# Layer 0 of a two-layer diffusion trunk: a third PSUM bank for attention scores, and projection work tied to its place among the attention tiles

## The chip, the core and the metric

The kernel runs on one core of a Trainium2 chip. The core has a matrix engine (PE in the profile; its weight loads have a row of their own, PEld), a vector engine (DVE), a scalar engine (ACT), GpSimd (POOL), and SyncE (SP), which issues most of the DMAs. Every engine works through its own list of instructions in order, and engines wait for one another by semaphores. PE writes its results to PSUM, which has eight banks of 128 x 512 fp32 values.

The metric is the device time of one execution in microseconds, lower is better.

## The reference, cut to what matters

Two layers work on 1024 latent tokens and 256 context tokens with 1024 features. Layer 0 (an "even" layer) projects the normalised, modulated tokens to queries, keys, values and gates, runs two groups of attention heads side by side, multiplies by a SiLU gate, and projects back:

```python
def even_mixer(h_lat, h_ctx, w_in, w_out, q_gain, k_gain, sink, cos, sin, update_ctx):
    ...
    aq, ak, av, ag, bq, bk, bv, bg = project(h_lat)
    c_aq, c_ak, c_av, c_ag, c_bq, c_bk, c_bv, c_bg = project(h_ctx)
    aq, ak, bq, bk = (apply_rope(t, cos, sin) for t in (aq, ak, bq, bk))
    ...
    oa = lax.map(lambda qb: gqa_attend(qb, ka, va), qa_blk)      # A: all keys
    ...
    ob = lax.map(b_block, (jnp.arange(n_blk), qb_blk))           # B: context and a band of keys, with a sink
    ...
    y_lat = jnp.concatenate([oa * jax.nn.silu(ag), ob * jax.nn.silu(bg)], axis=-1) @ w_out
```

Layer 1 (an "odd" layer) holds a depthwise convolution of 31 taps with a layer norm, and a two-dimensional neighbourhood attention with a table of biases. A final RMS norm gives the output.

## The kernel before

All products are fp32 values split in a high and a low part, so each logical product is three matmuls (`mm3`, lines 318 to 320: high by high, high by low, low by high). Attention in layer 0 is cut in four units `u`, each one key head with four query heads. `ORDER = (2, 3, 0, 1)`: first the two windowed B units, then the two global A units. A unit has ten groups of 128 queries (two of context, eight of latent tokens); a group is a run of key tiles, two to five in B and two or ten in A. Units 2, 3, 0, 1 have 42, 42, 84 and 84 tiles. In this text tiles are counted through the program: 0 to 41 for unit 2, 42 to 83 for unit 3, 84 to 167 for unit 0, 168 to 251 for unit 1, and 252 to 363 for the 16 groups of seven tiles of layer 1.

One tile is this chain: PE forms the score `st` in a PSUM bank, with one matmul over `QH` (line 465) and a second one over `QL` (line 469); ACT takes the exponential (`pf`, line 477) and its high part `ph` (line 296); POOL, or every twelfth time DVE, makes the low part `pl` (line 299); PE adds three matmuls to the output `ov` (lines 409 to 411). `attn_gen` issues the `ov` products of a tile three tiles behind its score (`LOOK0`). `QL` holds, beside the low parts of the queries, the negated row maxima, and these come from a preparation that runs beside earlier groups: matmuls into `mx` (lines 576, 588, 596), a maximum by DVE over each, `nmt`, a transpose on PE into `trn` (line 387), and a multiplication by DVE that writes `QL` (line 388). So the first `QL` matmul of a group needs its `trn` and the DVE step behind it.

The other work of layer 0 is fill for PE between the tiles: `proj_qkv` of the next unit (`pq`, ten blocks of 24 matmuls, then transposes `trk` into the layout of the keys in `qk_tail`), `proj_gate` (`pg`), and for the finished units the output products (`po`, `out0_part`). `weave` advances the attention generator `main` by `nmain` steps, two for a tile, and deals `nfill` steps of `fill` evenly among them. What it deals out is only a trace: a scheduler then orders each engine's list by priority and by its own estimate of when operands are ready. In layer 0 fill is traced with a priority 80 places later (`FL`), so the scheduler may move it far. `tc.issue_after(x)` adds an edge that keeps an instruction behind `x` on the same engine; `weave` has a parameter `lag` for it, which layer 0 does not use. In layer 1 fill has a priority 98 places earlier, and two of its four weaves use `lag`.

PSUM banks are shared out by tag: two for `pp` (projections), two for `mx`, two for `st`, one for `ov`, one for `tr`, which serves all small transposes and column sums (`trn`, `trm`, `trs`). The tag of `trk` is `tr` as well.

Weights come by DMA into `wr`, two buffers deep in layer 0, are cast by ACT to `wh` (line 296) and get their low part `wl` from POOL (line 299). The cast stands in ACT's list among the exponentials.

Of the kernel before, what the change touches and what calls it, by code (L numbers as in the profile page):

```python
# [41 lines left out]
TRV = "pp"  # L42
# [6 lines left out]
N0 = 9  # L49
NLAST = (48, 28)  # L50
PFB = 2
# [4 lines left out]
FL = (80, -98)  # L56
# [11 lines left out]
LATE = 100  # L68
NFILL = (34, 34, 34)
HV = (('gggvvvvg',) * 3, ('gggvvvvg', 'vvvgvvvg', 'gggvvvvg'))  # L70
O1 = (6, 84, 46, 14)
TICK0, TICK1 = (1, 3)
# [15 lines left out]
def tile_kernel(ctx: ExitStack, tc: tile.TileContext, a, out):  # L88
# [7 lines left out]

    BUFS = {"pp": 2, "mx": 2, "st": 2, "ov": 1, "tr": 1}
    solo = [True]
    turn = [0, 0]
    mk, mwp, hold, layer = [0], [None], [0], [0]  # L100
    sts, pvs = [], []

    def bank(tag, name):
# [65 lines left out]
    def mod_half(pool, l, part, j):  # L169

        pb = bank("pp", nm("pm"))
        c0 = part * 1024 + j * 512
        for d2 in range(4):
            w2 = mw_tile()
            mm0.append(SY.dma_start(w2, a["mod_w"][l, 2 * d2 * P : (2 * d2 + 2) * P, c0 : c0 + 512].rearrange("(d p) n -> p d n", d=2)))
            for d in range(2):
                dk = 2 * d2 + d
                PE.matmul(pb[0:2, :], csil[:, dk, :], w2[:, d, :], start=(dk == 0), stop=(dk == DK - 1))
        row = a0.tile([P, 512], F32, tag="ost", name=nm("mrow"), bufs=2)[0:2, :]
        SC.copy(row, pb[0:2, :])  # L180
        tr = bank("tr", nm("trm"))
        for i in range(4):
            PE.transpose(tr[:, 2 * i : 2 * i + 2], row[:, i * P : (i + 1) * P], ident[0:2, 0:2])
        trv = tr[:, 0:8].rearrange("p (i c) -> p i c", c=2)
        o = part * 8 + j * 4
        dst = modT[l][:, o : o + 4, :]
        VE.tensor_tensor(dst, trv, modb[:, l, o : o + 4, None].broadcast_to([P, 4, 2]), op=ALU.add)
        if part == 1:
            VE.scalar_tensor_tensor(gs[l][:, j * 4 : j * 4 + 4, :], dst, 1.0,
                                    normg[:, l, j * 4 : j * 4 + 4, None].broadcast_to([P, 4, 2]),  # L190
                                    op0=ALU.add, op1=ALU.mult)

    def mod_half_v(pool, l, part, j, conds):
# [28 lines left out]
        for n_, (q, t) in enumerate(zip(conds, accs)):  # L222
            tr = bank("ov" if solo[0] else "tr", nm("trm"))
            for i in range(4):
# [18 lines left out]

    def rstd_steps(pool, accs, n, tag, inv=1.0, tr="tr"):

# [68 lines left out]

    done = [None]

# [47 lines left out]
    def attn_prep(pool, g):  # L364
# [19 lines left out]
        for _ in range(3):  # L384
            yield
        tr2 = bank("tr", nm("trn"))
        PE.transpose(tr2[0:nr, 0:P], nmt[:, 0:nr].bitcast(F32), ident)
# [4 lines left out]
    def attn_gen(pool, groups, vshare, look, nexts=None):  # L392
# [57 lines left out]
        for x, (g, t) in enumerate(items):  # L450
# [13 lines left out]
            cs = slice(k * P, (k + 1) * P)  # L464
            sts.append(PE.matmul(st[:, :n], KA[:, cs], g.QH[:, q0 : q0 + n], start=True, stop=False))  # L465
            if not g.bias:
# [27 lines left out]

    def weave(main, nmain, fill, nfill, last=True, all_fill=True, lag=0):

        done = 0
        for k in range(nmain):
            next(main, None)
            while done * nmain < (k + 1) * nfill:  # L500
                with ExitStack() as cx:
                    cx.enter_context(later(FL[layer[0]]))
                    if lag and len(sts) >= lag:
                        cx.enter_context(tc.issue_after(sts[-lag].ins))
                    next(fill, None)
                done += 1
        if all_fill:
            for _ in fill:
                pass
        if last:  # L510
            for _ in main:
                pass
# [139 lines left out]
    with ExitStack() as p0x:  # L652
# [6 lines left out]
        with tc.tile_pool(name="st0", bufs=1, reuse_waits="tile") as st0:  # L659
# [31 lines left out]
            def norm_bc(c, acc):  # L691
                n = CHUNKS[c][1]
                return run(rstd_steps(st0, [acc], n, "st"))[:, :n]

# [139 lines left out]
        def qk_tail(u, j, pc):  # L834

            tr = bank("tr", nm("trk"))
            for i in range(3):
# [45 lines left out]
        for k in range(3):  # L883
            u = ORDER[k]
            n = NSTEP[u // 2] + (12 if k == 0 else 0)
            n0 = 0 if k else N0
            if not k:
                weave(main, n0, proj_gate(u, gblocks(k)[1]), 9, False)
            weave(main, n - n0 - NLAST[u // 2], fill0(k + 1), NFILL[k], False)
            weave(main, NLAST[u // 2], proj_gate(ORDER[k + 1], gblocks(k + 1)[1]), 18, False)  # L890
        run(mods)
# [78 lines left out]
    with tc.tile_pool(name="o0", bufs=1, reuse_waits="tile", side="right") as op_:  # L970
# [91 lines left out]

        weave(main, O1[0], load_oh(parts[0]), 6, False)
        weave(main, O1[1], out0_part(parts[0]), 48, False)
        weave(main, O1[2], chain(load_oh(parts[1]), out0_part(parts[1])), 30, False)
        ws = [load_w(op_, a["ev_wo"], e2 * 256, 256, 256, WO, lambda dk: "gv"[dk % 2], dks=final, rb=2) for e2 in range(4)]
        fp = [final_proj(c) for c in range(3)]
        nh = [norm_h(0, "st", "tr"), norm_h(1, "pp", "tr"), norm_h(2, "st", "tr")]
        weave(main, NSTEP[U1 // 2] - O1[0] - O1[1] - O1[2], through_attention(), O1[3])
        a0x.close()  # L1070
# [28 lines left out]
    with ExitStack():  # L1099
# [25 lines left out]
        def ln_steps(vp, c):  # L1125
# [25 lines left out]
            yield  # L1151
            bc = yield from rstd_steps(vp, [s1], 512, "st", 2.0)
            SC.copy(s2, bc)
# [480 lines left out]
```

## Time and profile before

| | |
|---|---|
| median of 3 runs | 1557.82 us (1554.83 to 1560.38) |
| the profiled execution | 1555.72 us |
| its span on the core | 1553.9 us |
| mean granted PE clock | 0.967 |
| busy share PE, PEld, DVE, ACT, POOL | 93%, 75%, 72%, 49%, 54% |
| first score of layer 0 | 159.4 us |
| first score of unit 3, unit 0, unit 1 | 325.8, 471.4, 685.9 us |
| first score of layer 1 | 1213.3 us |

The page names the busy time of each engine. A windows view cuts the span into stretches and gives, for each, its length and then the busy time of PE, PEld, DVE, ACT and POOL with the number of instructions in brackets, then the granted PE clock (PEclk, 1.00 is full speed), the share of the DMA engines and GB/s. With a line chosen it counts the instructions of that line alone. A waits view gives the engine and the tile that waited, what released it, the total, the number of times and the longest, all in us.

### The profile page before, as it was taken

The numbers are of one execution on the slowest core, as the hardware profiler recorded it, in microseconds if no ns is written. First come the engines' busy times: TensorE is split into PE (matmuls) and PEld (weight loads), VectorE is DVE, ScalarE is ACT, GpSimd is POOL, SyncE is SP. The second block draws the span as 40 slices with busy tenths as digits, with TensorE's granted clock in tenths as the row PEclk, the third lists the DMA queues.
The fourth block names the chain that finished last, engine by engine and source line by source line (L and its number), as shares of the span: only waits on it lengthen the run. The fifth ranks groups of instructions, "written<-read, shape, count | busy, mean of one in ns | idle before, by whom it ended". The sixth has DMA issues, their size and how long they took to land.

```text
span 1553.9 us, 22052 instructions
## 1 busy us (share of the span) xinstructions
PE 1449.1 (93%) x6984; PEld 1172.3 (75%) x6984; DVE 1123.3 (72%) x2172; ACT 759.8 (49%) x1545; POOL 833.5 (54%) x762
## 2 busy tenths in 40 slices
PE   6989989999999989899999889999999999799995
PEld 1878868887789678678887668888787787687784
DVE  4998898689858666654577677999755457586776
ACT  2721354445454755565455555443434455545563
POOL 1561464555555676675455666664542443545574
PEclk9999999999999999999999999999999999899996
DMA  9548245423441124631111121213456888788623
GB/s 339 194 146 270 79 125 174 147 64 121 151 129 44 54 89 143 207 115 56 42 45 35 68 95 57 80 63 123 158 178 222 272 225 263 221 264 240 192 92 109
DMA packets 185614, 221.01 MB, mean 142 GB/s; under 512 B 17421, under 2 KB 139481, under 8 KB 185497
## 3 DMA queue, kind: packets, MB, share of 16 engines
q1 hardware_dynamic: 178832, 208.03, 43.1%
q10 hardware_dynamic: 6664, 11.57, 2.3%
q8 instruction: 55, 0.90, 0.2%
q14 instruction: 63, 0.51, 0.1%
HBM read 159.51 MB, written 60.03 MB: 141 GB/s over the span
## 4 chain that ended last, share of the span: by engine, by line
PE 67%; DVE 12%; DMA 11%; issue 3%; POOL 3%; ACT 2%; SPq 2%; DVEq 0%; ACTq 0%; POOLq 0%
PE p L320 6%; PE p L318 6%; PE p L319 6%; PE ov L409 4%; PE ov L410 4%; PE ov L411 4%; PE st L465 4%; PE po L318 4%; PE st L469 4%; PE po L319 4%; PE po L320 4%; PE pq L320 2%; PE pq L319 2%; PE pq L318 2%; DMA mw<-in_mod_w_dram 2%
## 5 line engine op out<-in xcount | busy, mean ns | idle before, releaser
L299 POOL TENSOR_TENSOR pl<-pf,ph 128x512 fp32r<-128x512 f32 (+4 forms) x321 | 399.9, 1258 | 270.7 <-ACT ph L296 218.9
L299 POOL TENSOR_TENSOR wl<-wr,wh 128x256 fp32r<-128x256 f32 (+2 forms) x256 | 197.7, 788 | 227.9 <-ACT wh L296 203.3
L477 ACT ACTIVATE pf<-st 128x512 f32<-128x512 f32 x284 | 166.2, 596 | 161.7 <-PE st L469 106.3
L296 ACT CAST ph<-pf 128x512 fp32r<-128x512 f32 (+4 forms) x364 | 209.2, 588 | 25.5 <-PE ov L410 17.6
L296 ACT CAST wh<-wr 128x256 fp32r<-128x256 f32 (+2 forms) x264 | 103.2, 404 | 172.2 <-DMA wr<-in_od_d_dram 39.3
L318 PE MATMUL p<-hh,wh 128*128 128x512 f32 x448 | 177.7, 399 | 3.7 <-DVE spk L299 1.4
L319 PE MATMUL p<-hl,wh 128*128 128x512 f32 x448 | 177.9, 398 | 0.2 <-POOL hl L299 0.2
L320 PE MATMUL p<-hh,wl 128*128 128x512 f32 x448 | 175.2, 399 | 0.1
L465 PE MATMUL st<-QH,KAt 128*128 128x512 f32 (+4 forms) x364 | 144.0, 397 | 19.8 <-ACT pf L477 16.5
L409 PE MATMUL ov<-ph,Vt 128*128 128x512 f32 (+4 forms) x364 | 143.6, 394 | 8.8 <-DVE y L631 6.4
L411 PE MATMUL ov<-pl,Vt 128*128 128x512 f32 (+4 forms) x364 | 143.7, 395 | 3.9 <-POOL pl L299 3.8
L410 PE MATMUL ov<-ph,Vt 128*64 128x512 f32 (+4 forms) x364 | 140.8, 387 | 0.0
L469 PE MATMUL st<-QL,KBt 68*128 68x512 f32 (+4 forms) x364 | 138.2, 388 | 0.8 <-DVE QL L388 0.7
L1116 DVE SCALAR_TENSOR_TENSOR cps<-U,taps,cps 128x512 f32<-128x512 f32 x184 | 124.3, 747 | 0.0
L589 DVE TENSOR_REDUCE mp<-mx 128x1 f32<-128x512 f32 x128 | 85.5, 682 | 33.5 <-PE mx L588 32.7
L219 DVE SCALAR_TENSOR_TENSOR macc<-mw,csil,macc 128x512 f32<-128x512 f32 x107 | 97.5, 929 | 14.0 <-DMA mw<-in_mod_w_dram 13.2
L318 PEld LDWEIGHTS p<-hh,wh 128*128 128x128 f32 x448 | 84.6, 189 | 24.5 <-DVE spk L299 1.6
L465 PEld LDWEIGHTS st<-QH,KAt 128*128 128x128 f32 x364 | 69.8, 192 | 42.5 <-ACT pf L477 25.3
L319 PEld LDWEIGHTS p<-hl,wh 128*128 128x128 f32 x448 | 84.6, 189 | 20.4 <-POOL hl L299 0.6
L320 PEld LDWEIGHTS p<-hh,wl 128*128 128x128 f32 x448 | 84.6, 189 | 20.3 <-POOL wl L299 1.0
L411 PEld LDWEIGHTS ov<-pl,Vt 128*128 128x128 f32 x364 | 71.1, 195 | 28.1 <-POOL pl L299 7.6
L409 PEld LDWEIGHTS ov<-ph,Vt 128*128 128x128 f32 x364 | 71.5, 196 | 24.3 <-issue 7.0
(277 smaller groups left out, 3518.4 us busy)
## 6 DMA issues: line engine op xcount, KB each, us to landing
mw<-in_mod_w_dram SPq DMA_DIRECT2D x34, 512.0 KB, 5.6
bs<-in_d_bs_dram SPq DMA_DIRECT2D x16, 832.0 KB, 7.3
Q<-qs SPq DMA_DIRECT2D x40, 256.0 KB, 2.7
QH<-Q SPq DMA_DIRECT2D x80, 128.0 KB, 2.7
bm<-in_d_bm_dram SPq DMA_DIRECT2D x16, 540.0 KB, 6.1
wr<-in_od_d_dram SPq DMA_DIRECT2D x64, 128.0 KB, 2.6
mw<-in_mod_w_dram SPq DMA_DIRECT2D x28, 256.0 KB, 3.1
wr<-in_ev_qkv_dram SPq DMA_DIRECT2D x32, 192.0 KB, 3.8
```

Source lines behind the costliest of these rows:

```text
L296: SC.copy(hi, src)
L299: (GP if leng == "g" else VE).tensor_tensor(lo, src, hi.bitcast(F32), op=ALU.subtract)
L318: PE.matmul(o, lh, rh, start=first, stop=False)
L319: PE.matmul(o, lh, rl, start=False, stop=False)
L320: done[0] = PE.matmul(o, ll, rh, start=False, stop=last)
L409: PE.matmul(o, V[:, 64:192], ph[:, :n], start=(t == 0), stop=False)
L410: PE.matmul(g.ov[0:64, q0 : q0 + n], V[:, 0:64], ph[:, :n], start=False, stop=False)
L411: pvs.append(PE.matmul(o, V[:, 64:192], pl[:, :n], start=False, stop=(last and g.sink is None)))
L465: sts.append(PE.matmul(st[:, :n], KA[:, cs], g.QH[:, q0 : q0 + n], start=True, stop=False))
L469: PE.matmul(st[:, :n], KB[0:68, cs], g.QL[0:68, q0 : q0 + n], start=False, stop=True)
L477: SC.activation(pf[:, :n], st[:, :n], AF.Exp, scale=1.0 if g.bias else SCALE)
L1116: VE.scalar_tensor_tensor(pc, uc, w, pc, op0=ALU.mult, op1=ALU.add)
```

## The change

1. PSUM: the `tr` bank is given up and `st` gets three banks. The small transposes and sums move: `trn`, the late `trm` and layer 0's and layer 1's `trs` to the `mx` banks, the early `trm` and the norms at the start to `st`, `trk` to the `pp` banks (`TRV`), the layer norm's sums to `st`.
2. Order: in layer 0 fill gets edges. With `lag`, a step of fill stays behind the `lag`-th last score; that is the loose form, with 8, used in the first two units. With `tie` as well, a score stays behind the product of the second last step of fill; with `lag` 4 and `tie` 2 this is used while unit 0 and unit 1 run, except in the last stretch of unit 1.
3. Dealing: the steps of `weave` are split anew. `NLAST` is now by unit, unit 0 gives up its last 36 steps (`SHIFT`) to the output products of the units done before, and eight steps of the last projection are issued ahead of its weave (`NPRE`).

```diff
-NLAST = (48, 28)
+NLAST = (28, 28, 56)
...
+HOLD, TIE, LOOSE = 4, 2, 8
+NPRE = (0, 0, 8)
...
-O1 = (6, 84, 46, 14)
+O1 = (6, 110, 66, 14)
+SHIFT = 36
...
-    BUFS = {"pp": 2, "mx": 2, "st": 2, "ov": 1, "tr": 1}
+    BUFS = {"pp": 2, "mx": 2, "st": 3, "ov": 1}
...
-        tr2 = bank("tr", nm("trn"))
+        tr2 = bank("mx", nm("trn"))
...
-            sts.append(PE.matmul(st[:, :n], KA[:, cs], g.QH[:, q0 : q0 + n], start=True, stop=False))
+            with ExitStack() as cx:
+                if tied[0] is not None:
+                    cx.enter_context(tc.issue_after(tied[0].ins))
+                sts.append(PE.matmul(st[:, :n], KA[:, cs], g.QH[:, q0 : q0 + n], start=True, stop=False))
...
-    def weave(main, nmain, fill, nfill, last=True, all_fill=True, lag=0):
+    def weave(main, nmain, fill, nfill, last=True, all_fill=True, lag=0, tie=0):
...
+        past = []
         for k in range(nmain):
+            tied[0] = past[-tie] if tie and len(past) >= tie else None
             next(main, None)
+            tied[0] = None
             while done * nmain < (k + 1) * nfill:
...
                     next(fill, None)
+                past.append(prods[0])
                 done += 1
...
-            tr = bank("tr", nm("trk"))
+            tr = bank(TRV, nm("trk"))
...
-            n = NSTEP[u // 2] + (12 if k == 0 else 0)
+            n = NSTEP[u // 2] + (12, 0, -SHIFT)[k]
...
-            weave(main, n - n0 - NLAST[u // 2], fill0(k + 1), NFILL[k], False)
-            weave(main, NLAST[u // 2], proj_gate(ORDER[k + 1], gblocks(k + 1)[1]), 18, False)
+            hold = dict(lag=HOLD, tie=TIE) if k == 2 else dict(lag=LOOSE)
+            fill = fill0(k + 1)
+            for _ in range(NPRE[k]):
+                with later(FL[0]):
+                    next(fill)
+            weave(main, n - n0 - NLAST[k], fill, NFILL[k] - NPRE[k], False, **hold)
+            weave(main, NLAST[k], proj_gate(ORDER[k + 1], gblocks(k + 1)[1]), 18, False, **hold)
...
-        weave(main, O1[1], out0_part(parts[0]), 48, False)
-        weave(main, O1[2], chain(load_oh(parts[1]), out0_part(parts[1])), 30, False)
+        weave(main, O1[1], out0_part(parts[0]), 48, False, lag=HOLD, tie=TIE)
+        weave(main, O1[2], chain(load_oh(parts[1]), out0_part(parts[1])), 30, False, lag=HOLD, tie=TIE)
...
-        nh = [norm_h(0, "st", "tr"), norm_h(1, "pp", "tr"), norm_h(2, "st", "tr")]
-        weave(main, NSTEP[U1 // 2] - O1[0] - O1[1] - O1[2], through_attention(), O1[3])
+        nh = [norm_h(0, "st", "mx"), norm_h(1, "pp", "mx"), norm_h(2, "st", "mx")]
+        weave(main, NSTEP[U1 // 2] + SHIFT - O1[0] - O1[1] - O1[2], through_attention(), O1[3])
...
-            bc = yield from rstd_steps(vp, [s1], 512, "st", 2.0)
+            bc = yield from rstd_steps(vp, [s1], 512, "st", 2.0, "st")
```

The number and the shapes of the matmuls stay the same; only their order and their banks differ. Three places of PE's list show it. In the rows, the number behind a name tells tiles apart, and line numbers of the new kernel are a few higher (322 to 324 for the three products of `mm3`, 472 and 476 for the two matmuls of a score, 413 to 415 for `ov`, 391 for `trn`, 587 and 599 for `mx`).

Unit 0, tiles 96 to 99. Before, PE's list holds scores, maxima and outputs there and no projection:

```order
L465 MATMUL st_5355<-QH_4845,KAt_3729 128x512
L469 MATMUL st_5355<-QL_4846,KBt_1254 128x512
L411 MATMUL ov_5154<-pl_5289,Vt_1255 128x512
L588 MATMUL mx_5226<-KAt_3729,QH_4995 128x512
L465 MATMUL st_5388<-QH_4845,KAt_3729 128x512
L469 MATMUL st_5388<-QL_4846,KBt_1254 128x512
L588 MATMUL mx_5232<-KAt_3729,QH_4995 128x512
L465 MATMUL st_5410<-QH_4845,KAt_3729 128x512
L469 MATMUL st_5410<-QL_4846,KBt_1254 128x512
```

After, in the same place, a score is followed by a step of nine `pq` matmuls:

```order
L472 MATMUL st_5498<-QH_4845,KAt_3729 128x512
L476 MATMUL st_5498<-QL_4846,KBt_1254 128x512
L322 MATMUL pq_5577<-wh_5009,hh_171 128x384
L323 MATMUL pq_5577<-wl_5010,hh_171 128x384
L324 MATMUL pq_5577<-wh_5009,hl_172 128x384
L322 MATMUL pq_5577<-wh_5015,hh_171 128x384
L323 MATMUL pq_5577<-wl_5016,hh_171 128x384
L324 MATMUL pq_5577<-wh_5015,hl_172 128x384
L322 MATMUL pq_5577<-wh_5021,hh_171 128x384
```

What moved is the projection: before, tiles 90 to 113 stand with 8 `pq` matmuls among them; after, 120 do, and the stretches of six tiles with hardly any fill are tiles 114 to 119 (none) and 144 to 149 (nine `pg`). In units 2 and 3 every stretch of six tiles now has fill, where before tiles 6 to 11 and 48 to 59 had none.

The start of the third latent group of unit 0, at tile 104. Before, the transpose `trn` of the group's maxima stands well ahead of the group:

```order
L387 MATMUL trn_5297<-ident,nmt_5271 4x128
L409 MATMUL ov_5402<-ph_5413,Vt_1255 128x512
L410 MATMUL ov_5402<-ph_5413,Vt_1255 64x512
L411 MATMUL ov_5402<-pl_5414,Vt_1255 128x512
L409 MATMUL ov_5402<-ph_5436,Vt_1255 128x512
L410 MATMUL ov_5402<-ph_5436,Vt_1255 64x512
L465 MATMUL st_5491<-QH_4845,KAt_3729 128x512
L469 MATMUL st_5491<-QL_4846,KBt_1254 128x512
```

(The group's own first score follows twelve rows further down.) After, at the same tile:

```order
L324 MATMUL pq_5801<-wh_5021,hl_172 128x384
L391 MATMUL trn_5415<-ident,nmt_5389 4x128
L587 MATMUL mx_5508<-KAt_3729,QH_5418 128x256 x2
L587 MATMUL mx_5525<-KAt_3729,QH_5418 128x256 x2
L476 MATMUL st_5689<-QL_5131,KBt_1254 128x512
L476 MATMUL st_5710<-QL_5131,KBt_1254 128x512
L476 MATMUL st_5731<-QL_5131,KBt_1254 128x512
L472 MATMUL st_5755<-QH_5130,KAt_3729 128x512
L476 MATMUL st_5755<-QL_5131,KBt_1254 128x512
```

The three `QH` matmuls of tiles 104 to 106 stand further up, and their three `QL` matmuls now come together, two `mx` tiles (four matmuls of 256 columns) behind the `trn` on which they depend. Of the 40 groups of layer 0, 15 have no more than four such matmuls between `trn` and the first `QL` matmul in the new order, and one had before.

Layer 1, tile 292. Before, the fill is used up and the list goes on with outputs:

```order
L465 MATMUL st_13848<-QH_13204,KAt_12379 128x224
L469 MATMUL st_13848<-QL_13205,KBt_12380 128x224
L1226 MATMUL trv_14451<-ident,vc_14446 128x128 x2
L409 MATMUL ov_13802<-ph_13695,Vt_12386 128x512
L410 MATMUL ov_13802<-ph_13695,Vt_12386 64x512
L411 MATMUL ov_13802<-pl_13696,Vt_12386 128x512
```

After, projection products (`p`) stand there:

```order
L472 MATMUL st_13848<-QH_13204,KAt_12379 128x224
L476 MATMUL st_13848<-QL_13205,KBt_12380 128x224
L323 MATMUL p_3499_14080<-hl_9771,wh_13967 128x512
L324 MATMUL p_3483_14008<-hh_9770,wl_13980 128x512
L322 MATMUL p_3483_14008<-hh_9770,wh_13985 128x512
L323 MATMUL p_3483_14008<-hl_9771,wh_13985 128x512
```

What moved in layer 1: tiles 292 to 303 had no `p` matmul and now have 105; tiles 252 to 259 had 97 and now have 6.

More of the change, by code (lines that the diff above doesn't have):

```diff
@@ L101, in tile_kernel @@
     sts, pvs = [], []
+    tied = [None]
     def bank(tag, name):
@@ L180, in mod_half @@
         SC.copy(row, pb[0:2, :])
-        tr = bank("tr", nm("trm"))
+        tr = bank("st", nm("trm"))
         for i in range(4):
@@ L222, in mod_half_v @@
         for n_, (q, t) in enumerate(zip(conds, accs)):
-            tr = bank("ov" if solo[0] else "tr", nm("trm"))
+            tr = bank("ov" if solo[0] else "mx", nm("trm"))
             for i in range(4):
@@ L242, in newton_rsqrt, with rstd_steps @@
         return r
-    def rstd_steps(pool, accs, n, tag, inv=1.0, tr="tr"):
+    def rstd_steps(pool, accs, n, tag, inv=1.0, tr="mx"):
         nb = n // P
@@ L313, in make_h @@
                 split(x, h[0][:, dk, :], h[1][:, dk, :])
-    done = [None]
+    done = prods = [None]
     def mm3(o, lh, ll, rh, rl, first, last):
@@ L692, in norm_bc @@
                 n = CHUNKS[c][1]
-                return run(rstd_steps(st0, [acc], n, "st"))[:, :n]
+                return run(rstd_steps(st0, [acc], n, "st", tr="st"))[:, :n]
             made = [0]
```

## The prediction

> **What bounds the kernel now.** The page comes first.
>
> ```profile
> PE 1449.1 (93%) x6984; PEld 1172.3 (75%) x6984; DVE 1123.3 (72%) x2172; ACT 759.8 (49%) x1545; POOL 833.5 (54%) x762
> ```
>
> PE sets the pace, and the change leaves its work as it is, so it can gain only the time in which PE stands still or runs at a lower clock. I read the windows view next, cut where runs of projection matmuls begin and end. The columns are stretch, length, busy PE, PEld, DVE, ACT, POOL, then PEclk.
>
> ```profile
> core 0: us, PE busy (x) PEld busy (x) DVE busy (x) ACT busy (x) POOL busy (x), PEclk, DMA share, GB/s
> 470.00:505.00 35.00, 35.00 (x185) 31.66 (x184) 30.10 (x53) 13.66 (x25) 18.82 (x15) 1.00 0.16 49
> 505.00:544.00 39.00, 35.45 (x152) 24.52 (x151) 23.60 (x47) 28.64 (x50) 26.79 (x21) 1.00 0.18 54
> 544.00:556.00 12.00, 12.00 (x66) 11.19 (x65) 10.07 (x19) 6.17 (x13) 9.99 (x9) 1.00 0.28 90
> 556.00:580.00 24.00, 19.15 (x75) 13.33 (x74) 13.88 (x27) 13.77 (x28) 15.05 (x14) 0.86 0.27 80
> 580.00:637.00 57.00, 57.00 (x283) 46.25 (x282) 38.48 (x68) 32.91 (x59) 39.73 (x28) 1.00 0.42 134
> 637.00:652.00 15.00, 12.79 (x47) 8.54 (x46) 11.90 (x22) 8.97 (x14) 10.31 (x7) 0.89 0.86 260
> 652.00:685.00 33.00, 29.34 (x137) 22.72 (x138) 15.55 (x28) 21.55 (x40) 24.43 (x23) 1.00 0.58 183
> 685.00:875.00 190.00, 189.88 (x900) 152.47 (x899) 125.05 (x224) 97.73 (x185) 107.47 (x91) 1.00 0.17 55
> ```
>
> The same stretches with line 318 alone, the first of the three products of all fill:
>
> ```profile
> 505.00:544.00 39.00, 0.00 (x0) 0.00 (x0) 1.00 0.18 54
> 556.00:580.00 24.00, 0.00 (x0) 0.03 (x1) 0.86 0.27 80
> 637.00:652.00 15.00, 0.00 (x0) 0.00 (x0) 0.89 0.86 260
> 685.00:875.00 190.00, 53.43 (x148) 27.66 (x147) 1.00 0.17 55
> ```
>
> With fill evenly dealt, as from 685 to 875 us, PE idles 0.12 us in 190. Without fill it idles 3.55, 4.85 and 2.21 us in 78, though no other engine is full. The waits view of 470 to 685 us names the largest wait of PE, and one that sits behind it:
>
> ```profile
> PEld st L465 <- ACT pf L477: 11.1, 8, 2.7
> ACT wh L296 <- DMA wr<-in_ev_g_dram: 8.1, 5, 4.2
> ```
>
> The timeline shows how they meet (PE rows first, then ACT's):
>
> ```profile
> 557.78 0.40 PE L469 MATMUL st<-QL,KBt 68*128 68x512 f32 x1
> 558.02 0.39 PE L588 MATMUL mx<-KAt,QH 128*128 128x512 f32 x1
> 560.61 0.50 PE L465 MATMUL st<-QH,KAt 128*128 128x512 f32 x1 [2.19 <-ACT pf L477]
> 563.07 0.51 PE L576 MATMUL mx<-KAt,QH 128*128 128x256 f32 x2 [1.21 <-DVE mp L589]
> 565.24 0.63 PE L465 MATMUL st<-QH,KAt 128*128 128x512 f32 x1
> ...
> 559.14 0.40 ACT L296 CAST wh<-wr 128x256 fp32r<-128x256 f32 x1 [4.23 <-DMA wr<-in_ev_g_dram]
> 559.45 0.61 ACT L296 CAST ph<-pf 128x512 fp32r<-128x512 f32 x1
> 559.97 0.59 ACT L477 ACTIVATE pf<-st 128x512 f32<-128x512 f32 x1
> ```
>
> A weight cast stands in ACT's list ahead of an exponential and waits 4.23 us for its DMA; both score banks are full; PE stands 2.19 us, and what follows runs at a lower clock (0.63 us a matmul against 0.40). Fill, or a third bank, would cover this.
>
> **Part 1, unit 0 (470 to 685 us).** The three stretches without fill lose 3.55 + 4.85 + 2.21 = 10.6 us of idling, and by the clock 0.14 x 24 + 0.11 x 15 = 5.0: 15.6 us. The scores in them are
>
> ```profile
> 505.00:544.00 39.00, 9.49 (x23) 4.32 (x23) 1.00 0.18 54
> 556.00:580.00 24.00, 4.36 (x9) 1.94 (x9) 0.86 0.27 80
> 637.00:652.00 15.00, 2.86 (x6) 1.23 (x6) 0.89 0.86 260
> ```
>
> 38 tiles, 0.41 us each. In the new order 12 tiles of unit 0 have next to no fill: 12 x 0.41 = 4.9 us stay. From 652 to 685 us output products have begun but 3.66 us are idle; I give the even dealing half, 1.8. Gain 15.6 - 4.9 + 1.8 = 12.5 us. The least is 6 (half), the most all 19.3.
>
> Idling as PE's rows show it may understate the loss, because a matmul's row (0.39) is longer than the step to the next (558.02 - 557.78 = 0.24). By weight loads, full PE means 152.47 / 190 = 0.80, so the three stretches did 24.52 + 13.33 + 8.54 = 46.4 us of loads, worth 58 us, in 78: 20 lost instead of 15.6. The Trainium skill (Perfetto Trace Analysis, Identifying the Most-Contended Engine) has this as a rule: judge PE by weight loads, since matmul busy time hides pipelining. By that rule the sum below would end 4.5 us lower; the trace agrees in direction, and since the mix of shapes sets the 0.80 too, I keep the idle time.
>
> **Part 2, units 2 and 3 (182 to 470 us).**
>
> ```profile
> 182.00:212.00 30.00, 26.26 (x116) 18.48 (x115) 27.53 (x65) 18.87 (x44) 17.34 (x14) 0.89 0.24 71
> 238.00:341.00 103.00, 101.84 (x546) 89.29 (x545) 77.33 (x167) 46.16 (x98) 52.47 (x42) 1.00 0.44 134
> 341.00:372.00 31.00, 27.19 (x122) 18.76 (x121) 28.34 (x66) 17.81 (x41) 17.82 (x14) 1.00 0.28 83
> 384.00:394.00 10.00, 7.98 (x39) 5.74 (x39) 9.82 (x18) 5.29 (x15) 5.72 (x6) 1.00 0.41 123
> 394.00:470.00 76.00, 73.39 (x376) 61.98 (x375) 52.39 (x110) 36.00 (x74) 42.30 (x35) 0.98 0.44 136
> ```
>
> The stretches of 30, 31 and 10 us, almost without fill, lose 3.74 + 3.81 + 2.02 us and 0.11 x 30 = 3.3 by the clock: 12.9. But here DVE is over 90% busy, where it is 75% and 69% in the two filled ones. Spreading fill spreads DVE's load too, yet the loose edges still let a group's maxima bunch up. I take 8, with ends 0 and 13.
>
> **Part 3, the price at group starts.** In 15 of 40 groups the new order puts `trn` at most two `mx` tiles ahead of the first `QL` matmul. The chain is in the timeline:
>
> ```profile
> 539.24 0.27 PE L387 MATMUL trn<-ident,nmt 128*4 128x128 f32 x1
> 539.54 0.68 DVE L388 TENSOR_TENSOR QL<-trn,k_bd 4x512 fp32r<-4x512 f32 x1 [1.52 <-PE trn L387]
> ```
>
> From `trn` to the end of DVE's step are 0.98 us, and PE starts 0.05 after a releaser (560.61 against 559.97 + 0.59). Between stand the `trn` (0.11, my estimate from its 128 columns) and four matmuls of 256 columns (half of 0.24 each): 0.59. So PE waits at least 0.44 us, and 0.68 more for each other DVE step queued ahead. Then three scores finish at once, and the fourth needs the first one's exponential (0.59). I take 0.6 us a group, 15 x 0.6 = 9 lost; the ends are 7 (the chain alone) and 45 (rival 1). `trn` in the `mx` banks and `trk` in the `pp` banks cost no work of their own; the attention matmuls around them hide their evacuation, else 0.68 a `trn` is part of that upper end.
>
> **Part 4, layer 1.** No edge is added here, but with the third bank the fill stands elsewhere.
>
> ```profile
> 1332.00:1362.00 30.00, 21.43 (x89) 15.99 (x88) 16.62 (x44) 15.95 (x34) 14.66 (x17) 0.77 0.88 235
> PEld mx L1342 <- DMA KAt<-KD: 3.5, 1, 3.5
> ```
>
> This stretch, tiles 292 to 303 in the main, loses 8.6 us idle and 0.23 x 30 = 6.9 by the clock: 15.5. The wait for a load of keys (3.5 us, second row, from the waits of this stretch) stays, with about as much for clock: 6.5. Tiles 252 to 262 lose their fill instead: 11 x 0.41 = 4.5. Gain 15.5 - 6.5 - 4.5 = 4.5; the ends are -5, if the old loss stays beside the new one, and 13.
>
> The start (to 159 us), the end of layer 0 and the tail have the same work in much the same order; I cost them at nothing, within 3 us either way.
>
> **The sum.** The profiled execution took 1555.7 us, 2.1 under the median. 1555.7 - 12.5 - 8 + 9 - 4.5 = 1539.7; with 2.1 added back, a median of **1542 us**, 1.0% faster.
>
> **Rivals.**
> 1. *Group starts become the bound: slower.* PE works strictly down its list, so nothing passes a waiting `QL` matmul. If DVE has three maxima (0.68 each) queued ahead, a start costs 0.44 + 2.0 + 0.59 = 3.0 us, 45 in all: 1555.7 - 25 + 45 = 1576, median 1578. It decides against the change above 25 / 15 = 1.7 us a group. For it: DVE at 92% without fill. Against: it is at 66% from 685 to 875 us. The clock matters here: two waits of 2.19 and 1.21 us close together brought PEclk to 0.86, while 3.55 us in small pieces left it at 1.00. The Trainium skill (TensorE: Matmul & The Clock Gate, The HAM clock gate) puts the limit at an idle window of about 3.4 us, by which single starts of 3 us would still cost no clock; the trace's case agrees only if the two waits count as one.
> 2. *The gaps only move.* Fill is a fixed amount; what one stretch gets another lacks (tiles 114 to 119, 144 to 149, 252 to 262). For it: ACT's weight casts still wait two buffers deep. Against: the 0.12 us above. With part 1 at its least and parts 2 and 4 at nothing: 1555.7 - 6 + 9 = 1559, median 1561.
> 3. *Full packing.* All of 19.3 + 13 + 13, and starts at 7: 1555.7 - 45.3 + 7 = 1517, median 1519. For it: the stretch from 685 to 875 us. Against: DVE's load in units 2 and 3.
>
> **How the numbers follow.** Forecast 0.66, rival 1 0.16, rival 2 0.10, rival 3 0.08. With each gain halfway to its ends (16 + 10.5 + 9, or 9 + 4 + 0) the forecast's own range is 1531 to 1554. Rival 3 opens the range to 1517, rival 2 to 1562; rival 1 is left out. About 0.3% (4.7 us) is what a measurement can tell from no change. Faster 0.66 + 0.08 = 0.74, same 0.10, slower 0.16.
>
> **What would show it.** Right: PE idle under 6 us in all of unit 0, PEclk 1.00 there, no ACT wait of over 2 us on a gate weight, and waits of `st` on DVE's `QL` near 9 us in total. Wrong: waits on `QL` or on maxima of over 25 us, or a layer 1 longer than before.

## The result, and the profile after

The changed kernel takes 1631.3 us (median of 4 runs, 1626.8 to 1634.2) against 1558.1 us (1554.8 to 1560.4) on the same chip: a ratio of 1.047, with a 95% interval of 1.0435 to 1.0503. The forecast was 1542 us, faster; the kernel is 73 us slower, above rival 1's 1578 too.

The profiled execution has a span of 1624.9 us, 71 longer. Its page has the same work, PE busy for 30 us more, at a mean granted clock of 0.946 against 0.967, and so idle for 41 us more:

```profile
PE 1479.4 (91%) x6984; PEld 1194.2 (73%) x6984; DVE 1127.6 (69%) x2172; ACT 763.4 (47%) x1545; POOL 836.2 (51%) x762
```

The windows view, cut at the first score of the program, of unit 0 and unit 1, at tile 246, at the first score of layer 1 and at the end, shows where. Columns: stretch, length, busy PE, PEld, DVE, ACT, POOL with counts, PEclk, DMA share, GB/s. First the kernel before:

```profile
159.00:472.00 313.00, 297.31 (x1517) 249.31 (x1516) 250.84 (x539) 149.19 (x332) 170.96 (x139) 0.98 0.39 120
472.00:686.00 214.00, 199.73 (x931) 157.18 (x931) 142.75 (x257) 124.67 (x225) 144.10 (x113) 0.98 0.37 115
686.00:889.00 203.00, 197.74 (x931) 157.48 (x930) 132.06 (x236) 106.06 (x200) 116.38 (x99) 0.99 0.16 50
889.00:1213.00 324.00, 314.08 (x1447) 253.93 (x1446) 236.73 (x391) 143.63 (x285) 174.96 (x179) 0.99 0.38 123
1213.00:1553.00 340.00, 305.48 (x1494) 249.18 (x1493) 233.43 (x547) 177.89 (x381) 168.98 (x178) 0.94 0.70 209
```

And after:

```profile
165.00:516.00 351.00, 309.03 (x1508) 259.45 (x1507) 244.00 (x535) 146.37 (x328) 169.72 (x137) 0.92 0.36 108
516.00:742.00 226.00, 209.67 (x966) 164.52 (x965) 146.98 (x257) 126.50 (x231) 150.72 (x120) 0.96 0.34 108
742.00:941.00 199.00, 194.13 (x903) 153.46 (x901) 129.00 (x233) 105.62 (x193) 110.53 (x92) 0.99 0.17 50
941.00:1277.00 336.00, 317.14 (x1433) 254.10 (x1432) 241.88 (x395) 145.63 (x288) 174.79 (x179) 0.97 0.37 117
1277.00:1624.00 347.00, 311.09 (x1510) 254.74 (x1508) 236.96 (x547) 180.70 (x384) 171.46 (x181) 0.93 0.68 206
```

More than half of the loss is in units 2 and 3: 313 us became 351, for about as many matmuls (1517 and 1508). PE's idle time there rose from 15.7 to 42.0 us, and its busy time by 12 us for nine matmuls fewer, while the clock fell from 0.98 to 0.92. The start and unit 0 lost 6 and 12, the end of layer 0 with the convolution 12, layer 1 lost 7, and unit 1 gained 4; the new order puts 35 more matmuls in unit 0 and 28 fewer in unit 1, so these two are best read together.

These are single profiles, and a stretch has a spread of its own. In kernels below whose PE list is there the same as in the kernel before, or the same but for a few rows, the first score came 158.0 to 163.7 us into the span (165.3 here), units 2 and 3 took 311 to 314 (351 here), tile 246 to layer 1 took 324 to 333 (336 here), and layer 1 took 335 to 342 (348 here). Only the 38 us are far outside.

What ends the idle time in units 2 and 3 (PE's weight loads, waits view of 159 to 471 us before, its three largest):

```profile
PEld st L465 <- ACT pf L477: 9.5, 11, 2.3
PEld mx L596 <- DVE mp L578: 3.7, 3, 1.8
PEld mx L576 <- DMA QH<-Q: 2.3, 1, 2.3
```

and of 165 to 516 us after:

```profile
PEld trn L391 <- DVE nmt L387: 25.2, 8, 5.7
PEld mx L587 <- DVE QL L392: 8.4, 6, 3.4
PEld mx L607 <- DVE mp L589: 4.7, 5, 2.1
...
PEld st L472 <- ACT pf L484: 2.9, 6, 0.6
```

The old wait is down from 9.5 to 2.9. A new one, of PE at `trn`, is much larger. The timeline of one of the eight shows what PE waits for (the PE row first, then DVE's list):

```profile
249.10 0.38 PE L391 MATMUL trn<-ident,nmt 128*12 128x128 f32 x1 [4.84 <-DVE nmt L387]
...
244.49 0.92 DVE L423 STREAM_TRANSPOSE r<-ov 64x256 f32<-64x256 f32 x2
245.44 0.57 DVE L608 CUSTOM_DVE_ANT_0 mx<-mx,k_bm 128x384 f32<-128x384 f32 x1
246.03 0.08 DVE L608 DVE_READ_ACCUMULATOR2_ANT mp<- 128x1 f32 x1
246.03 0.55 DVE L303 TENSOR_TENSOR qs<-trk,qs 128x384 fp32r<-128x384 f32 x1
246.50 0.19 DVE L425 RECIPROCAL r<-r 128x8 f32<-128x8 f32 x1
246.61 0.12 DVE L381 TENSOR_REDUCE nmt<-mp 128x4 fp32r<-128x12 f32 x1
246.73 0.45 DVE L426 STREAM_TRANSPOSE rb<-r 128x256 f32<-128x256 f32 x1
247.10 0.12 DVE L384 SCALAR_TENSOR_TENSOR se<-nmt,sink 128x4 f32<-128x4 f32 x1
247.21 0.85 DVE L642 TENSOR_TENSOR y<-ov,rb 64x256 f32<-64x256 f32 x2
248.08 0.56 DVE L303 TENSOR_TENSOR qs<-trk,qs 128x384 fp32r<-128x384 f32 x1
248.56 0.41 DVE L644 SCALAR_TENSOR_TENSOR y<-y,gt 128x256 f32<-128x256 f32 x1
248.89 0.15 DVE L387 TENSOR_TENSOR nmt<-se,nmt 128x4 fp32r<-128x4 f32 x1
```

DVE does not stand still. The last maximum of the group (line 608) and the three small steps to `nmt` (lines 381, 384, 387) are spread through its list among the steps that finish another group (423 to 426, 642, 644) and those of queries and keys (303), and PE has come to the `trn` 4.84 us too early. The second row is of another kind. The matmuls of line 587 read `KAt` and `QH`; of `QL` and `trn` they need nothing. The longest of these waits (PE, then DVE):

```profile
264.12 0.27 PE L391 MATMUL trn<-ident,nmt 128*12 128x128 f32 x1
264.14 0.48 PE L587 MATMUL mx<-KAt,QH 128*128 128x256 f32 x2
267.80 0.50 PE L587 MATMUL mx<-KAt,QH 128*128 128x256 f32 x2 [3.18 <-DVE QL L392]
...
265.67 0.42 DVE L344 SCALAR_TENSOR_TENSOR sg<-sg,pg 128x256 f32<-128x256 f32 x1 [3.63 <-ACT sg L343]
266.12 0.92 DVE L423 STREAM_TRANSPOSE r<-ov 64x256 f32<-64x256 f32 x2
267.07 0.68 DVE L392 TENSOR_TENSOR QL<-trn,k_bd 12x512 fp32r<-12x512 f32 x1
```

By the code `trn` has one of the two `mx` banks and the first pair of these matmuls the other. The second pair starts when DVE's `QL` step has read `trn`, and that step stands in DVE's list behind one of a gate projection, which waits 3.63 us for ACT, and one that finishes another group. Everything behind the pair in PE's list waits too. In the kernel before, no maximum waits for a `QL` step.

Windows around the two waits show what the clock did:

```profile
241.10:244.50 3.40, 1.67 (x10) 0.86 (x8) 3.37 (x9) 1.19 (x3) 1.65 (x3) 1.00 0.35 118
244.50:249.10 4.60, 0.00 (x0) 0.00 (x1) 4.43 (x14) 1.19 (x5) 2.26 (x2) 0.50 0.58 171
249.10:254.70 5.60, 5.31 (x16) 4.02 (x17) 2.69 (x5) 2.64 (x6) 1.90 (x2) 0.50 0.74 233
265.00:268.40 3.40, 0.60 (x4) 0.56 (x5) 2.63 (x6) 0.63 (x2) 0.00 (x0) 1.00 0.21 71
268.40:275.20 6.80, 6.80 (x26) 5.80 (x25) 4.81 (x11) 3.92 (x11) 2.77 (x2) 0.50 0.29 83
```

In the first case the clock fell to half already as the wait of 4.84 us began, behind a stretch in which PE was busy for 1.67 of 3.40 us; it was still at half for the 5.6 us of work behind the wait. In the second, half the clock lasted for the 6.8 us behind the wait.

### The profile page after: what moved, and what is told of

Read it like the earlier page. It is cut to its first block, busy times and chain, and to the rows that moved or that the text cites. A ratio compares the mean times of both kernels' runs of the same rounds, so it can differ in the third digit from the quotient of the medians.

```text
span 1624.9 us, 21962 instructions
## 1 busy us (share of the span) xinstructions
PE 1479.4 (91%) x6984; PEld 1194.2 (73%) x6984; DVE 1127.6 (69%) x2172; ACT 763.4 (47%) x1545; POOL 836.2 (51%) x762
## 4 chain that ended last, share of the span: by engine, by line
PE 63%; DVE 16%; DMA 10%; issue 5%; POOL 3%; ACT 2%; SPq 1%; ACTq 0%; DVEq 0%; POOLq 0%
PE p L322 6%; PE p L323 6%; PE p L324 6%; PE st L476 4%; PE st L472 4%; PE po L322 4%; PE po L323 4%; PE po L324 3%; PE ov L415 3%; PE ov L413 3%; PE ov L414 3%; PE pq L324 2%; PE pq L322 2%; PE pq L323 2%; DVE macc L223 2%
## 5 line engine op out<-in xcount | busy, mean ns | idle before, releaser
L322 PE MATMUL pq<-wh,hh 128*128 128x384 f32 x256 | 89.1, 348 | 2.3 <-ACT pc L813 2.2
```

Source lines behind the costliest of these rows:

```text
L322: PE.matmul(o, lh, rh, start=first, stop=False)
```

## The experiments

All ratios are to the kernel before, measured beside each kernel; 1% is 15.6 us. A "ring" is the set of PSUM banks of one tag, which its tiles take in turn. "Close start" means a group start with at most about 1 us of PE work between `trn` and its first `QL` matmul in the list.

| kernel | median us | ratio | 95% interval |
|---|---|---|---|
| changed | 1631.3 | 1.0469 | 1.0435 to 1.0503 |
| banks_only | 1619.2 | 1.0368 | 1.0318 to 1.0418 |
| seven | 1614.2 | 1.0334 | 1.0296 to 1.0372 |
| trn_mx | 1592.8 | 1.0202 | 1.0170 to 1.0234 |
| trn_own | 1577.8 | 1.0131 | 1.0099 to 1.0162 |
| mx3 | 1584.8 | 1.0165 | 1.0131 to 1.0199 |
| old_banks | 1579.1 | 1.0108 | 1.0067 to 1.0149 |
| old_tied | 1558.1 | 1.0000 | 0.9976 to 1.0024 |
| old_tie1 | 1568.7 | 1.0059 | 1.0034 to 1.0083 |
| v110 | 1559.8 | 0.9994 | 0.9977 to 1.0011 |
| v111h8 | 1568.6 | 1.0057 | 1.0038 to 1.0077 |
| no_loose | 1617.4 | 1.0369 | 1.0314 to 1.0424 |
| only_loose | 1618.8 | 1.0384 | 1.0330 to 1.0439 |
| trn_st | 1640.4 | 1.0502 | 1.0461 to 1.0542 |
| banks_trn_st | 1621.9 | 1.0397 | 1.0349 to 1.0445 |
| after_noexp | 1625.0 | 1.0419 | 1.0394 to 1.0444 |
| before_noexp | 1583.1 | 1.0148 | 1.0125 to 1.0172 |
| null_vs13 | 1566.3 | 1.0040 | 1.0015 to 1.0065 |
| null_fl40 | 1564.5 | 1.0024 | 1.0006 to 1.0041 |

### Banks or edges

The banks alone (on the kernel before):

```diff
-    BUFS = {"pp": 2, "mx": 2, "st": 2, "ov": 1, "tr": 1}
+    BUFS = {"pp": 2, "mx": 2, "st": 3, "ov": 1}
...
-        tr2 = bank("tr", nm("trn"))
+        tr2 = bank("mx", nm("trn"))
```

with the other users of `tr` moved as in the change.

> The kernel before with the new banks alone: three score banks, no tr bank, trn and late trm in the mx banks, trk in the pp banks; no edges in layer 0, dealing as before. In the order of PE's list 3 of the 40 group starts of layer 0 have no more than two mx products between trn and the first QL matmul (15 in the changed kernel, 1 before). Theory 1, group starts (the transpose trn and the DVE step behind it are put just in time, and each close start costs about 5 us with the clock: 73 us for 14 more): 1558 + 10 = 1568 us. Rival A, the edges cost all and the bank helps: 1545 to 1558. Rival B, trn and trk have lost their own bank and must wait for, and hold up, the maxima: close to the changed kernel, 1610 to 1630.

The changed kernel with the banks of before, that is this diff backwards:

> The changed kernel with the banks of before (two st banks, one tr bank for trn, trk, trm, trs), edges and dealing as changed. 6 close starts instead of 15. Theory 1: 1558 + 25 = 1583 us. Rival A, the edges cost all: 1600 to 1630. Rival B, the lost tr bank costs all: 1545 to 1560.

Measured 1.0368 and 1.0108. The banks cost most, as rival B says; the edges alone cost 1.1% (17 us), less than theory 1's 25 and between the two rivals. The count of close starts is no measure: the banks alone have three and lose 57 us. The new dealing has no run of its own, without any edge. In `old_tie1` below, which has edges in unit 1 alone, PE's list of units 2 and 3 is row for row that of the kernel before, so there the dealing does nothing by itself.

The edges apart, on the changed kernel; without the loose ones:

```diff
-            hold = dict(lag=HOLD, tie=TIE) if k == 2 else dict(lag=LOOSE)
+            hold = dict(lag=HOLD, tie=TIE) if k == 2 else {}
```

> The changed kernel without the loose edges of the first two units (2 and 3); three score banks, dealing and the edges of units 0 and 1 stay. 10 close starts, of which 3 in units 2 and 3 (8 in the changed kernel). Theory 1: units 2 and 3 give back some 25 of the 39 us that they grew by, 1631 - 25 = 1606 us. Rival A, the loose edges themselves (fill that is kept back delays the next unit's keys) cost the 39 us: 1592 or less. Rival B, the banks: 1620 to 1631.

and with the loose ones alone (`{}` where `k == 2`, and no `lag` and `tie` in the two output weaves):

> The changed kernel with the loose edges of units 2 and 3 alone, without edges and ties in units 0 and 1; three score banks. 8 close starts, all in units 2 and 3. Theory 1: the 39 us of units 2 and 3 stay and unit 0 gives back its 11: 1631 - 18 = 1613 us, with units 0 and 1 as in the kernel with the banks alone. Rival A: about the same, 1600 to 1615. Rival B: 1620 to 1631.

Measured 1.0369 and 1.0384. Without the loose edges the time is that of the banks alone: the ties cost and gain nothing that could be told from the intervals, and the loose edges cost 16 us beside the ties. By themselves they show only 2 us over the banks alone, within the intervals; so this 16 is not a sum that holds in every company, and why the loose edges cost is not shown.

### Which part of the banks

All small tiles moved as in the change, but two score banks, the eighth bank empty:

```diff
-    BUFS = {"pp": 2, "mx": 2, "st": 3, "ov": 1}
+    BUFS = {"pp": 2, "mx": 2, "st": 2, "ov": 1}
```

> The kernel before with all small transposes and sums moved to the mx, st and pp banks as in the change, but still two score banks; the eighth bank stays empty. 7 close starts (trn at most 1.1 us of PE work ahead of the first QL matmul). Theory 2, trn in a ring with the maxima (a maximum waits for the DVE step behind trn, and trn for a maximum): most of the 57 us of the banks alone are here, 1590 to 1620 us. Theory 3, the third score bank itself (PE takes three QH products early and then stands with three open scores): near the kernel before, 1555 to 1575.

The kernel before with `trn` alone moved to the `mx` banks:

> The kernel before with trn alone moved to the mx banks; two score banks, and the tr bank serves trk, trm and trs. Theory 2 (trn among the maxima): 1580 to 1610 us. Theory 3 (the third score bank): 1555 to 1570. If what matters is trk in the pp banks, it is 1555 to 1565 as well, and the kernel with seven banks is then slower than this one.

The reverse, `trn` alone left in a `tr` bank of its own, with `trk`, `trm` and `trs` moved:

> The kernel before (two score banks, no edges) with the eighth bank kept for trn alone; trk moves to the pp banks, trm and trs to the st and mx banks as in the change. With trn moved alone the time was 32 us over the kernel before, with all of them moved 54. Theory 2, the lost bank, trn first (costs add up): 1560 + 21 = 1581 us. Rival, trk, trm and trs matter only together with trn in the mx banks: 1560 to 1565. Rival, the costs come from whatever order the scheduler happens to find, and don't add: anything between 1560 and 1615.

And the freed bank given to the maxima:

```diff
-    BUFS = {"pp": 2, "mx": 2, "st": 3, "ov": 1}
+    BUFS = {"pp": 2, "mx": 3, "st": 2, "ov": 1}
```

> The kernel before with all small transposes and sums moved as in the change, and the freed bank given to the maxima: three mx banks, two st banks. Theory 2a, the mx ring is short (a trn holds one of two banks until its DVE step has run, and the maxima have one left): with three the cost of trn goes, and with it that of trm and trs, 1560 to 1580 us. Theory 2b, any ring that trn shares costs, since its banks are handed out in program order and DVE serves both: as with seven banks, 1600 to 1615.

Measured 1.0334, 1.0202, 1.0131 and 1.0165. `trn` in the maxima's ring costs 2.0%, the other small tiles 1.3%, both together 3.3%: they add up. The third score bank on top (1.0368 against 1.0334) gains nothing. A third bank in the ring that `trn` shares gives half of the 3.3% back, a time between the ranges of 2a and 2b. So theory 3 falls and theory 2 holds here; a longer ring takes back most of what `trn` costs, and the rest of the small tiles costs besides.

The wait at `trn` is large where all small tiles share the two-bank ring. PE's weight loads in units 2 and 3, of the kernel with seven banks, with three `mx` banks, and with `trn` in its own bank:

```profile
PEld trn L387 <- DVE nmt L383: 14.3, 6, 4.7
```

```profile
PEld trn L387 <- DVE nmt L383: 4.0, 4, 1.5
```

```profile
PEld trn L387 <- DVE QL L388: 3.0, 2, 1.5
PEld trn L387 <- DVE nmt L383: 1.0, 3, 0.4
```

But with `trn` alone in the ring the same row reads

```profile
PEld trn L387 <- DVE nmt L383: 1.3, 2, 0.8
```

and that kernel still loses 2.0%, in other places: of the 37 us by which its profile is longer, 18 lie between the first score and tile 246 and 11 in layer 1, whose groups share the ring too. So the wait at `trn` is the form that the cost takes in some of the lists.

The wait of a maximum for the `QL` step does follow the ring. It is there in each of the eight kernels with `trn` in the `mx` ring (in layer 0, 14.1 us in the changed kernel, 6.1 with the banks alone, 4.4 with seven banks, 3.2 with three `mx` banks, 3.0 with `trn` alone moved) and in none of the others. In `trn_own`, `trn` itself waits for an earlier `QL` step, 3.0 us in the third fence above. So a tile in the ring is held up by the DVE step that empties the bank of another. With `trn` alone moved that is 3.0 of the 31 us.

The rest is open, and the order of the list is a rival for it. Where `trn` shares the ring and no edge holds the fill, the scheduler moves fill forward: between the first scores of units 2 and 0 stand 1851 matmuls with `trn` alone moved, 1791 with seven banks and 1599 with three `mx` banks, against 1494 with `trn` in its own bank and 1517 before. No run has the new banks with the old order, so what the waits cost and what the other order costs is not told apart. Nor is it shown which of `trk`, `trm` and `trs` makes the 1.3%.

### Is it the late trn?

`trn` in the three score banks instead of the `mx` banks, in the changed kernel and in the one with the banks alone:

```diff
-        tr2 = bank("mx", nm("trn"))
+        tr2 = bank("st", nm("trn"))
```

> The changed kernel with trn in the score banks in place of the mx banks: three st banks that trn shares, edges and dealing as changed. PE's list then holds no close start in units 0 to 3 (15 in the changed kernel) and one or two open scores at a start where there were three. Theories 1 and 2 (late trn, trn among the maxima): 40 to 70 us come back, 1560 to 1590. Theory 3 (the third score bank itself): 1615 to 1631. If the cause is trk in the pp banks or the edges, 1610 to 1631.

> The kernel with the new banks alone (no edges), with trn in the three score banks in place of the mx banks. No close start in units 0 to 3. Theories 1 and 2: 1545 to 1575 us, against 1619 for the banks alone. Theory 3: 1600 to 1620. By the prediction's own gains a third score bank with early trn should beat the kernel before: 1535 to 1555.

Measured 1.0502 and 1.0397: no gain, though no start in units 0 to 3 is close. Theory 1 (the number of close starts sets the cost) falls. Theory 2 missed too: its 40 to 70 us did not come back. Units 2 and 3 together went from 351 to 329 us by their first scores in the changed kernel, but the first score came 14 us later (178.8 against 165.3; 190.2 against 164.9 with the banks alone) and the stretch from tile 246 to layer 1 grew by 19. In this ring the maxima no longer wait for a `QL` step, and the time is lost all the same, so `trn` beside scores costs as well; by what path is not shown.

The two exponentials of the sink out of the way, in the changed kernel and before (these two kernels leave out the sink's weight in the output):

```diff
-            SC.activation(nmt[:, 4:8], se, AF.Exp)
-            SC.activation(se, se, AF.Exp)
+            VE.tensor_copy(nmt[:, 4:8], se)
```

> The changed kernel without the two exponentials of the sink in the preparation of a B group (line 385 and 386): DVE copies the argument in their place, so that ACT has no step between the maxima and trn; the sink's weight in the output is left out with it. Theory 6, PE stands at trn because these two steps wait in ACT's list behind weight casts and exponentials (trn waited 25 us for nmt of line 387 in units 2 and 3): that wait falls below 5 us, units 2 and 3 get 20 to 30 us shorter, 1601 to 1612 us. Rival, the shared ring makes trn late and the exponentials only carry the name: the wait moves to another step of the chain (nmt, QL, mx), 1622 to 1631.

> The same edit on the kernel before, as a control, the sink's weight left out: there trn has its own bank and hardly waits (under 1 us in units 2 and 3). Theory 6: 1553 to 1560 us, no gain beyond the 40 short ACT steps. Rival (the exponentials cost wherever they stand): 1535 to 1548.

Measured 1.0419 and 1.0148. In the first, PE's wait at `trn` in units 2 and 3 is much as in the changed kernel (25.2):

```profile
PEld trn L390 <- DVE nmt L386: 24.5, 8, 5.8
```

Theory 6 falls: these ACT steps are not the link that is late, and what is left of the chain is DVE's list, as the timeline shows. The second kernel, the control, is 23 us slower with 40 ACT steps fewer, outside both ranges. Why is open.

### Is it only another list?

That control made it possible that any new list costs some 20 us. Two changes of one number, `VS0` from 12 to 13 and `FL` from `(80, -98)` to `(40, -98)`, on the kernel before:

> The kernel before with one number changed that takes nothing away and adds nothing: every 13th low part of an exponential goes to DVE in place of every 12th (two of 252 change engine in layer 0). The scheduler then writes another list for layer 0 (about half of PE's rows in units 2, 3, 0 and 1 stand elsewhere) and the same one for layer 1. Theory 7, the list before is a good one among many, and another list of the same work costs some 20 us (as the kernel without the sink's exponentials, 23 slower with less work): 1573 to 1585 us. Rival, the list matters little and the cost of the other kernels was that of their banks and edges: 1555 to 1565 us.

> The kernel before with fill in layer 0 traced 40 priority places later in place of 80: the same work and banks and no edges, another list for layer 0 and the same for layer 1. Theory 7: 1570 to 1585 us. Rival: 1555 to 1565 us.

Measured 1.0040 and 1.0024. For these two lists theory 7 falls: they cost 4 to 6 us, not 20, and differences below 0.5% between the kernels above say nothing on banks or edges. Two lists are not all lists, and the control stays unexplained. But all kernels that took small tiles out of their own bank are 1.3% to 5.0% slower, while those with the old banks and without loose edges, the control apart, are within 0.6% of the kernel before.

### Can a part of it gain?

The old banks with edges in units 0 and 1 only:

> The banks of before, the new dealing, and edges only where units 0 and 1 run (lag 4, tie 2); no loose edges in units 2 and 3, whose list is then the same as before. Theory 4, the loose edges cost 23 us in unit 2 (the time that PE lost there went from 18 to 42 us in the run with the old banks) and the ties gain some 6 in unit 1: 1553 to 1557 us. Rival, the ties cost as much as the loose edges: 1565 to 1579.

The same with edges in unit 1 only:

> The banks of before, the new dealing, and edges only while unit 1 runs (output products); none in units 2, 3 and 0. With three score banks the ties in unit 0 went with 13 us more of lost PE time and those in unit 1 with 7 less. By that: 1552 to 1556 us, faster than the kernel before and than with ties in unit 0 as well. Rival, the prediction's part 1 (ties in unit 0 gain 12): slower than with ties in both.

With edges in unit 0 and in the first output stretch of unit 1:

> The banks of before, the new dealing, edges (lag 4, tie 2) while unit 0 runs and in the first output stretch of unit 1 only; PE's list of units 2 and 3 and of layer 1 is then that of the kernel before but for a few rows. The ties gain 7 us in unit 1 (lost PE time 10.5 before, 3.6 tied) and nothing in unit 0: 1549 to 1555 us, the first that could beat the kernel before. Rival, the 7 us are within the spread of single profiles: 1556 to 1561.

With looser ones:

```diff
-HOLD, TIE, LOOSE = 4, 2, 8
+HOLD, TIE, LOOSE = 8, 3, 8
```

> As the kernel before with old banks and ties in units 0 and 1, but looser: lag 8 and tie 3, in all stretches; layer 1's list is that of the kernel before. If the form of the tie matters little: 1549 to 1556 us. If the tighter tie is what holds the fill in unit 1: as the kernel before, 1556 to 1562.

Measured 1.0000, 1.0059, 0.9994 and 1.0057: none beats the kernel before, and all four missed the range that was expected for a gain. Without the loose edges the 1.1% of `old_banks` is gone, so these cost 17 us with the old banks, as they did beside the ties in the changed kernel. The ties do what they are meant to in unit 1 (windows of units 0 and 1, the old banks with both tied):

```profile
471.00:695.00 224.00, 213.67 (x982) 169.93 (x981) 146.86 (x262) 125.20 (x229) 147.22 (x117) 0.95 0.35 111
695.00:881.00 186.00, 185.72 (x881) 148.53 (x879) 123.67 (x224) 105.25 (x193) 111.02 (x92) 1.00 0.17 52
```

PE idles 0.3 us in unit 1, against 5.3 before. In unit 0 it idles 10.3 against 14.3, but the clock is 0.95 against 0.98. What is gained there is of the size of the differences between lists, and does not show in the total.

## Why the prediction was wrong, step by step

- *What bounds the kernel* (PE, its idle time and clock): right. The loss is idle time of PE (41 of 71 us) and longer busy time at a lower clock.
- *Part 1, unit 0, gain 12.5.* Wrong. In the changed kernel PE idles 16.3 us there against 14.3, with 966 matmuls against 931, and the clock fell from 0.98 to 0.96. With the old banks the same ties leave 10.3 idle and no gain in the total.
- *Part 2, units 2 and 3, gain 8, ends 0 and 13.* Wrong in sign. The loose edges cost 17 us with the old banks. The prediction had read DVE at over 90% in the stretches without fill as a limit on the gain; it did not allow for a loss there.
- *Part 3, the price at group starts, 9 us, ends 7 and 45.* This is the step that failed. "`trn` in the `mx` banks and `trk` in the `pp` banks cost no work of their own; the attention matmuls around them hide their evacuation": together with `trm` and `trs`, which moved as well and were given no term of their own, they cost 3.3%, 52 us, of which `trn` alone 2.0% (31 us) and the rest 1.3% (20 us). What the 9 us did price, scores that wait for the `QL` step, came to 9.1 us in 8 waits (2.4 before); that this fits is partly luck, since it was worked out as 15 starts of 0.6. What was put at nothing is that a tile in a shared ring waits for the step that empties another's bank (maxima behind `trn`: 14.1 us in 11 waits, none before), and that PE can stand at `trn` itself for the DVE steps ahead of it: 25.2 us in 8 waits, up to 5.7, where the row used had DVE's step right behind `trn`. How the 52 us divide among such waits and the other order stays open.
- *The third score bank.* It was worth nothing in the total (1.0368 against 1.0334). The wait of `st` on `pf` in units 2 and 3, 9.5 us before, is 2.0 with the banks alone, but it is 3.6 with seven banks as well, where `st` has two: most of its fall is not the third bank's doing. The largest wait of PE by name was not where a bank was worth most.
- *Part 4, layer 1, gain 4.5.* Wrong by sign: 340 us became 347, just past the lower end of -5, and a longer layer 1 was one of the named signs of being wrong. Little can be made of the 7 us: single profiles that share one list of layer 1 go from 335 us (v110) to 342 (old_banks), 341 before. With `trn` alone moved it was 352, with seven banks 351, so the ring seems to cost there too.
- *Start, end of layer 0, tail, "nothing, within 3".* Not borne out, by less than it looks: 6 us at the start and 12 between unit 1 and layer 1, of which the spread of one list covers up to 4 and 9.
- *Rival 1* had the side and the kind of mechanism (PE waits at group starts, in order) and its sign was the right one, at a chance of 0.16. Its price rested on scores that wait for a `QL` step behind queued maxima; those waits came to 9.1 us in the whole program. The larger ones are of maxima on the `QL` step (14.1) and of PE one step earlier, at `trn` (25.2). Its 45 us were too few.
- *The clock.* The wait of 3.18 us that ends at 267.8 stands in a window with PEclk 1.00, and the 6.8 us behind it ran at 0.50. The Trainium skill (TensorE: Matmul & The Clock Gate, The HAM clock gate) puts the limit at an idle window of about 3.4 us; here a wait slightly under it, alone, was followed by a low clock, so the prediction's sentence that single starts of 3 us cost no clock by that rule is not borne out.

The runs divide the loss as 52 (lost bank) + 5 (third bank, no more than another list costs) + 0 (ties) + 16 (loose edges) = 73 us. That this meets the measured 73 is no check: each term is the step from one kernel to the next (seven, banks_only, no_loose, changed). Each ratio is known to some 5 to 9 us, so only the 52 and the 16 are clear of noise.

## What to carry to other kernels

A PSUM bank for small transposes looks idle, but it keeps apart chains that would otherwise wait for one another; before it is given up, price the ring that its users move to, with every engine that must empty that ring. Take the wait that a trace names as the largest for what it is worth in the total only after a run that removes it. Where a scheduler fills gaps by its own estimate, edges that spread the fill evenly are not free: the loose ones cost 16 to 17 us here, and the ties lowered PE's idle time in unit 1 (5.3 to 0.3 us) without a gain in the total.

## What was not expected of the hardware

A wait of 3.18 us was followed by half the clock for 6.8 us, and shorter ones were too. In the kernel before:

```profile
642.00:645.40 3.40, 1.69 (x4) 0.56 (x3) 3.39 (x8) 3.02 (x5) 2.66 (x2) 1.00 0.88 308
645.40:648.80 3.40, 3.39 (x8) 2.50 (x9) 2.66 (x5) 1.21 (x2) 3.40 (x3) 0.50 0.79 198
```

The longest wait of PE in the first row is 1.10 us, but PE was busy for only half of it, and the next 3.4 us ran at half the clock. In the changed kernel the row from 241.1 us, busy for 1.67 of 3.40, was followed by the same. In these cases several short waits did what one long one does.

Over the program the mean clock went from 0.967 to 0.946, and in units 2 and 3 the longer busy time of PE was about a third of the loss (12 of 38 us). And the list has a spread of its own: nearly the same work, with the same banks and edges, took 0.2% to 0.4% more in another order.
